# Splitting weights in steps of 1024 columns in place of 512

## The chip, the cores and the metric

The kernel runs on one core of one Trainium2 chip. The metric is the device time of one execution in microseconds (us). Its engines go by the names of the profile: PE (TensorE, the matmuls, with PEld its weight loads), DVE (VectorE), ACT (ScalarE), POOL (GpSimd) and SP (SyncE, which issues the weight DMAs).

## The reference

A trunk of four decoder layers on a sequence of 256 tokens, width 1024, all in float32. Each layer has three sub-layers, and after each of them stands `x = layer_norm(ALPHA * x + f(x))`:

```python
for i in range(DEPTH):
    kind, j = i % N_MIXERS, i // N_MIXERS
    if kind == 0:
        y = swa_sink_attention(x, a_w_qkv[j], a_sinks[j], a_w_o[j], cos_a, sin_a)
    elif kind == 1:
        y = rglru_block(x, b_w_in[j], b_conv_w[j], ...)
    else:
        y = mla_attention(x, c_w_down[j], c_q_norm[j], ...)
    x = layer_norm(ALPHA * x + y, ln_g[i, 0], ln_b[i, 0])
    x = layer_norm(ALPHA * x + memory_cross_attention(x, mem_k, mem_v, x_w_q[i], x_w_o[i]), ...)
    x = layer_norm(ALPHA * x + conv_glu_ffn(x, f_w_up[i], f_conv_w[i], f_conv_b[i], f_w_down[i]), ...)
```

The mixers are a sliding-window attention of 16 heads in 4 groups with learned sinks (layers 0 and 3), a recurrent block with real gates, the RG-LRU (layer 1), and a latent attention (layer 2). Cross-attention has 4 heads over 256 memory tokens; the FFN has 2816 gated channels with a causal convolution of width 3.

## The kernel before, in words

**Weights in two parts.** A float32 product is built from three matmuls on rounded operands: each weight and each activation is split into a high part and a low part, the difference, and high by high, high by low and low by high are summed in PSUM (`mm3`). For activations `split` (L370, L371) does this: a copy on ACT writes the high part (`xh`, `oh`, `ph`, `gh`), a subtract on DVE the low part (`xl`, `ol`, `pl`, `gl`). For weights it is the class `Weights`. `PLAN` lists the weights in pieces, most of 2048 columns on 128 partitions (1 MB), in the order in which they are used. `load` starts the DMA of a piece into one of `NRAW` = 3 buffers (`raw`) on SP's queue; `step` splits the next columns of the piece at hand: a cast on ACT into `whi` (L287), then a subtract on DVE into `wlo` (L288). There are `NSPLIT` = 4 pairs of `whi` and `wlo`; a piece's first step waits until `free` has given a pair back, that is, until PE has used it. With a piece's last step its raw buffer is given back and the next load is issued.

**When a step is issued.** The matmuls on weights go through `bulk`, which adds each one's columns / 2.4 to a credit (`tick`). When the credit has reached `STEP_NS` and no `hold` stands, one step is issued and `STEP_NS` taken off. The credit is capped at twice `STEP_NS`:

```python
def tick(self, ns):
    self.ns = min(self.ns + ns, 2 * STEP_NS)
    if self.ns >= STEP_NS and not self.hold and self.step():
        self.ns -= STEP_NS
```

`get` also issues steps, where a piece is asked for that isn't split yet. The size of a step is `PART` columns, or what is left of the piece; the first two pieces of all have sizes of their own (`FIRST`). At the end of a sub-layer `OutProj.finish` sets `hold` during the norm, so that no step is issued into its chain.

**The order of the rest.** Within a sub-layer the work of all engines is written out in short stages, and strings of tokens (`SWA_SEQ`, `RG_SEQ`, `MLA_SEQ`, `X_SEQ`), played by `play`, set the order of the stages: in the sliding window `K` turns the keys (copies to `kT`, L773), `R` applies the rotation (`ropet`, `ropeu`, L685 to L689), `U` turns the queries (`qT`, L699), `S` makes the scores, their row maxima on DVE (L722), the sink's maximum and its negative (L725, L726) and the exponentials on ACT (L731), `N` normalizes (L737 to L740), `T` turns the probabilities (`pt`, L750), `P` multiplies them with the values and splits the result into `oh` and `ol`, `C` is a part of the output projection. Cross-attention has the same stages, with the row maxima at L1090, the exponentials at L1093, and queries (`q`) and probabilities (`ph`, `pl`) split as well; `mkh`, `mvh` and their low parts are the memory's keys and values. All engines run their own instructions in order. A scheduler at build time orders them for each engine from the order of issue and its own estimate, so that a change in the steps can also move other instructions.

The change and the steps of the prediction touch `Weights.step` and `Weights.tick` with their two constants, L239 and L329; `bulk`, which calls `tick`, is at L354.

Of the kernel before, what the change touches and what calls it, by code (L numbers as in the profile page):

```python
# [235 lines left out]
MORE_REST = ((0, 2, 4), (1, 0, 4))  # L236
NRAW = 3
NSPLIT = 4
PART = 512  # L239


class Weights:
# [28 lines left out]
    def step(self):  # L271
# [9 lines left out]
        hi, lo = self.tiles[k]  # L281
        c = slice(self.part, FIRST[k][self.part] if k < 2 else min(n, self.part + PART))
        raw = self.raw[k]
# [39 lines left out]
# [3 lines that stand above are left out]
            self.ns -= STEP_NS  # L326


STEP_NS = 1200.0  # L329
XF_AT = 4  # L330
FIRST = [{0: 256, 256: 512, 512: 1024, 1024: 1536, 1536: 2048}, {0: 512, 512: 1024, 1024: 2048}]

# [945 lines left out]
```

## Time and profile before

| what | value |
|---|---|
| three runs, median (lowest to highest) | 1385.0 us (1384.55 to 1385.14) |
| the profiled execution | 1384.68 us |
| its span, first to last instruction | 1382.7 us |
| mean granted clock of TensorE | 0.999 |
| busy: PE, PEld | 99%, 89% of the span |
| busy: DVE, ACT | 78%, 64% of the span |
| DMA read over the span | 244 MB, 177 GB/s |

The times are those of the whole execution; the span leaves out what lies before the first and after the last instruction, 2.0 us here. "Busy" is the time in which an engine had an instruction in work; matmuls are pipelined, so a busy PE is not yet a PE at its peak. A granted clock of 1 is 2.4 GHz. In a timeline row the number in brackets is the idle time of the engine just before the instruction, and what ended it; a row with x4 stands for four instructions in a row, and its duration reaches from the first one's start to the last one's end.

### The profile page before, as it was taken

The page shows a single profiled execution, that of the slowest core. Times are in us where ns is not written, and L with a number is a line of the kernel's source. Part 1 is how long each engine was busy: PE and PEld are TensorE (multiplying, and loading weights), DVE is VectorE, ACT ScalarE, POOL GpSimd, SP SyncE. Part 2 cuts the span into 40 slices and gives each one's busy share as a digit, 9 for nine tenths or more (in the row PEclk, how much of TensorE's full clock was granted, in tenths as well). Part 3 has the DMA queues.
Part 4 walks back from the last instruction along what each step waited for, and adds up shares of the span by engine and source line. Part 5 has one row for each costly group of instructions (what it writes and reads, how often), then busy time and mean ns, then how long its engine had stood idle before and what let it go on. Part 6 is the DMA issues. An engine that isn't in the chain of part 4 may idle for free.

```text
span 1382.7 us, 23749 instructions
## 1 busy us (share of the span) xinstructions
PE 1363.8 (99%) x9110; PEld 1232.0 (89%) x9110; DVE 1084.8 (78%) x2392; ACT 881.1 (64%) x1892; POOL 13.0 (1%) x28
## 2 busy tenths in 40 slices
PE   8999999999999999999999999999999999999997
PEld 8887989999898898999988898999998789899996
DVE  6887869777788878877778687977779867797775
ACT  6666747555579666655557664855565856675553
POOL 0000000000000000000000000000000000000000
PEclk9999999999999999999999999999999999999999
DMA  8733536555535554655526442555554326455550
GB/s 319 273 137 122 203 104 246 205 189 183 183 123 184 199 196 168 225 187 183 179 103 236 153 176 99 214 214 185 192 195 148 135 94 228 166 214 183 185 182 31
DMA packets 39393, 246.78 MB, mean 178 GB/s; under 512 B 4336, under 2 KB 6640, under 8 KB 12400
## 3 DMA queue, kind: packets, MB, share of 16 engines
q1 hardware_dynamic: 35824, 232.69, 46.3%
q0 software_dynamic: 3456, 12.58, 2.7%
q8 instruction: 71, 1.16, 0.3%
q14 instruction: 42, 0.34, 0.1%
HBM read 244.21 MB, written 1.05 MB: 177 GB/s over the span
## 4 chain that ended last, share of the span: by engine, by line
PE 92%; ACT 3%; DVE 3%; issue 0%; DMA 0%; SPq 0%; DVEq 0%; ACTq 0%
PE ps L352 89%; PE ps L359 3%; ACT p L731 2%; DVE p L722 1%; DVE wlo L288 1%; DMA raw<-in_w_dram 0%; DVE tt L834 0%; ACT whi L287 0%; DVE x L478 0%; DVE x L480 0%; DVE x L454 0%; DVE tt L832 0%; ACT oh L370 0%; ACT tt L861 0%; DVE ropet L689 0%
## 5 line engine op out<-in xcount | busy, mean ns | idle before, releaser
L288 DVE TENSOR_TENSOR wlo<-raw,whi 128x512 fp32r<-128x512 f32 (+1 forms) x869 | 559.1, 683 | 149.5 <-ACT whi L287 143.0
L287 ACT CAST whi<-raw 128x512 fp32r<-128x512 f32 (+1 forms) x869 | 485.9, 619 | 174.6 <-PE ps L352 150.2
L352 PE MATMUL ps<-xh,whi 128*128 128x256 f32 x1504 | 421.2, 280 | 0.0
L352 PE MATMUL ps<-xh,wlo 128*128 128x256 f32 x1504 | 420.1, 279 | 0.0
L352 PE MATMUL ps<-xl,whi 128*128 128x256 f32 x1504 | 419.8, 279 | 0.0
L352 PEld LDWEIGHTS ps<-xl,whi 128*128 128x128 f32 x1504 | 282.7, 188 | 1.9
L352 PEld LDWEIGHTS ps<-xh,whi 128*128 128x128 f32 x1504 | 282.7, 188 | 1.8
L352 PEld LDWEIGHTS ps<-xh,wlo 128*128 128x128 f32 x1504 | 282.6, 188 | 0.0
L1151 DVE SCALAR_TENSOR_TENSOR cv<-ps,part,cv 128x255 f32<-128x255 f32 (+1 forms) x352 | 166.3, 477 | 3.8 <-ACT cv L1149 1.4
L352 PE MATMUL ps<-whi,xh 128*128 128x512 f32 (+3 forms) x336 | 118.4, 353 | 0.4 <-ACT xh L370 0.2
L352 PE MATMUL ps<-wlo,gh 128*128 128x512 f32 x352 | 116.0, 396 | 0.0
L352 PE MATMUL ps<-whi,gh 128*128 128x512 f32 x352 | 115.9, 396 | 0.0
L352 PE MATMUL ps<-wlo,xh 128*128 128x512 f32 (+3 forms) x336 | 115.7, 345 | 0.0
L352 PE MATMUL ps<-whi,gl 128*128 128x512 f32 x352 | 115.1, 393 | 0.0
L1149 ACT ACTIVATE cv<-ps,part 128x256 f32<-128x256 f32 x176 | 98.3, 563 | 16.9 <-DVE cv L1151 5.5
L370 ACT CAST gh<-cv 128x256 fp32r<-128x256 f32 x88 | 35.7, 406 | 107.2 <-DVE cv L1166 107.0
L352 PE MATMUL ps<-whi,oh 128*128 128x512 f32 x256 | 92.9, 403 | 3.4 <-ACT oh L370 3.4
L352 PE MATMUL ps<-whi,xl 128*128 128x512 f32 (+3 forms) x336 | 92.6, 347 | 0.0
L352 PE MATMUL ps<-wlo,oh 128*128 128x512 f32 x256 | 90.8, 394 | 0.0
L352 PE MATMUL ps<-whi,ol 128*128 128x512 f32 x256 | 90.6, 395 | 0.0
L352 PEld LDWEIGHTS ps<-whi,gl 128*128 128x128 f32 x352 | 66.3, 188 | 15.8
L352 PEld LDWEIGHTS ps<-wlo,gh 128*128 128x128 f32 x352 | 66.4, 189 | 15.3
(227 smaller groups left out, 1842.1 us busy)
## 6 DMA issues: line engine op xcount, KB each, us to landing
raw<-in_w_dram SPq DMA_DIRECT2D x210, 1024.0 KB, 4.8
lng<-in_ln_g_dram POOLq DMA_DIRECT2D x12, 512.0 KB, 4.5
lnb<-in_ln_b_dram POOLq DMA_DIRECT2D x12, 512.0 KB, 6.2
raw<-in_w_dram SPq DMA_DIRECT2D x5, 768.0 KB, 4.7
raw<-in_w_dram SPq DMA_DIRECT2D x5, 256.0 KB, 6.1
raw<-in_w_dram SPq DMA_DIRECT2D x2, 640.0 KB, 3.7
xf<-in_xT_dram SPq DMA_DIRECT2D x1, 1024.0 KB, 8.6
x<-in_x_dram SPq DMA_DIRECT2D x1, 1024.0 KB, 13.2
```

The source lines that it names most:

```text
L287: self.nc.scalar.copy(out=hi[:, c], in_=raw[:, c])
L288: self.nc.vector.tensor_tensor(out=lo[:, c], in0=raw[:, c], in1=hi[:, c].bitcast(F32), op=ALU.subtract)
L352: T.matmul(o, lhsT=l, rhs=r, start=st, stop=sp, **kw)
L359: T.transpose(o, i, ident)
L370: a = A.copy(out=hi, in_=src)
L722: V.tensor_tensor_reduce(out=pr[:, hd], in0=sc[e][:, c], in1=mk, scale=1.0, scalar=-3e38, op0=ALU.add, op1=ALU.max, accum_out=m[:, tb, hd: ...
L731: last[0] = A.activation(out=pr[:, hd], in_=pr[:, hd], func=AF.Exp, scale=A_D ** -0.5, bias=nm[:, b, hd:hd + 1], accum_out=sm[:, b, hd:hd ...
L1149: A.activation(out=dst, in_=src, func=AF.Identity, scale=wc[:, taps - 1:taps], bias=bias)
L1151: V.scalar_tensor_tensor(out=dst[:, d:], in0=src[:, :S - d], scalar=wc[:, taps - 1 - d:taps - d], in1=dst[:, d:], op0=ALU.mult, op1=ALU.add)
```

## The change

Two constants are doubled: the columns of a split step and the credit at which one is issued. A piece of 2048 columns takes two steps instead of four; one of 1536 takes 1024 and 512, one of 1280 takes 1024 and 256. The cap on the credit, which is written as twice `STEP_NS`, doubles with it.

```diff
--- before.py
+++ after.py
@@ -236,7 +236,7 @@
 MORE_REST = ((0, 2, 4), (1, 0, 4))
 NRAW = 3
 NSPLIT = 4
-PART = 512
+PART = 1024
 
 
 class Weights:
@@ -326,7 +326,7 @@
             self.ns -= STEP_NS
 
 
-STEP_NS = 1200.0
+STEP_NS = 2400.0
 XF_AT = 4
 FIRST = [{0: 256, 256: 512, 512: 1024, 1024: 1536, 1536: 2048}, {0: 512, 512: 1024, 1024: 2048}]
```

How this moves instructions is seen at two places. The first is VectorE at the beginning of the sliding window in layer 0, the difference of the orders; `wlo` is a split step, the rest the rotation of the queries:

```order
 L689 TENSOR_TENSOR ropet<-ropet,ropeu 128x512
-L288 TENSOR_TENSOR wlo<-raw,whi 128x512 x3
+L288 TENSOR_TENSOR wlo<-raw,whi 128x1024
 L685 TENSOR_TENSOR ropet<-ps,cont 128x512
 L687 TENSOR_TENSOR ropeu<-ps,cont 128x8x32 x2
-L288 TENSOR_TENSOR wlo<-raw,whi 128x512
+L288 TENSOR_TENSOR wlo<-raw,whi 128x1024
 L689 TENSOR_TENSOR ropet<-ropet,ropeu 128x512
```

Nothing has changed places here, but the single step between the rotation's products and their sum, and so ahead of the row maxima that follow, has grown from 512 columns to 1024. In the same layer, on the same engine, the row maxima of the third group end in this way before:

```order
L288 TENSOR_TENSOR wlo<-raw,whi 128x512
L725 SCALAR_TENSOR_TENSOR m<-m,sinkt 128x8
L722 ISA p_1186,m<-ps,cont 128x128
L722 ISA m 128x1
L726 TENSOR_SCALAR nm<-m 128x8
L727 TENSOR_TENSOR es<-sinkt,m 128x8
```

and in this way with the change:

```order
L288 TENSOR_TENSOR wlo<-raw,whi 128x1024
L725 SCALAR_TENSOR_TENSOR m<-m,sinkt 128x8
L722 ISA p_1126,m<-ps,cont 128x128
L722 ISA m 128x1
L726 TENSOR_SCALAR nm<-m 128x8
L727 TENSOR_TENSOR es<-sinkt,m 128x8
```

The step ahead of the sink's maximum is 1024 columns long, where it had 512. The second place is the cross-attention of layer 0. On ScalarE:

```order
 L370 CAST ph<-ps 128x512
 L1093 ACTIVATE xp,xsm<-ps,xnm 128x256 x2
-L287 CAST whi<-raw 128x512
+L287 CAST whi<-raw 128x1024
+L370 CAST ph<-ps 128x512
 L370 CAST q<-ps 128x512
-L370 CAST ph<-ps 128x512
-L287 CAST whi<-raw 128x512 x2
-L370 CAST oh<-ps 128x512
-L370 CAST ph<-ps 128x512
-L287 CAST whi<-raw 128x512
+L287 CAST whi<-raw 128x1024
```

The cast behind the exponentials has twice the columns, and the probabilities' high part now comes ahead of the query's. TensorE follows that in the same place:

```order
 L352 MATMUL ps<-mkh,q 128x256
 L352 MATMUL ps<-mkl,q 128x256
+L352 MATMUL ps<-ph,mvh 128x256
+L352 MATMUL ps<-pl,mvh 128x256
+L352 MATMUL ps<-ph,mvl 128x256
+L352 MATMUL ps<-ph,mvh 128x256
+L352 MATMUL ps<-pl,mvh 128x256
+L352 MATMUL ps<-ph,mvl 128x256
+L352 MATMUL ps<-ph,mvh 128x256
 L352 MATMUL ps<-mkh,q 128x256 x2
 L352 MATMUL ps<-mkl,q 128x256
```

Seven matmuls on the probabilities stand behind the first two on the queries, where they followed all of these.

## Rows read from the trace of the kernel before

**Rows 1.** The page, parts 1 and 4: busy time, and the chain by engine.

```profile
PE 1363.8 (99%) x9110; PEld 1232.0 (89%) x9110; DVE 1084.8 (78%) x2392; ACT 881.1 (64%) x1892; POOL 13.0 (1%) x28
...
PE 92%; ACT 3%; DVE 3%; issue 0%; DMA 0%; SPq 0%; DVEq 0%; ACTq 0%
```

**Rows 2.** Windows: us, then busy us and count by engine, PEclk, DMA share, GB/s.

```profile
83.00:112.00 29.00, 27.15 (x210) 21.43 (x209) 26.57 (x109) 25.84 (x90) 0.00 (x0) 1.00 0.29 105
428.00:448.00 20.00, 18.32 (x131) 16.62 (x129) 16.45 (x28) 18.31 (x31) 0.00 (x0) 1.00 0.30 111
211.00:380.00 169.00, 169.00 (x1194) 157.65 (x1193) 133.32 (x268) 105.62 (x216) 0.00 (x0) 1.00 0.55 198
```

**Rows 3.** Waits of PE: line <- releaser: us, times, longest us.

```profile
PE ps L352 <- ACT whi L287: 5.0, 2, 4.2
PE ps L352 <- ACT oh L370: 3.4, 4, 1.2
PE ps L359 <- DVE p L740: 1.9, 4, 0.5
```

**Rows 4.** The page, part 5: the group of the subtracts.

```profile
L288 DVE TENSOR_TENSOR wlo<-raw,whi 128x512 fp32r<-128x512 f32 (+1 forms) x869 | 559.1, 683 | 149.5 <-ACT whi L287 143.0
```

**Rows 5.** Timeline of ACT, then DVE, near the start: start us, us, operation.

```profile
15.23 1.05 ACT L287 CAST whi<-raw 128x1024 fp32r<-128x1024 f32 x1
16.44 2.19 ACT L287 CAST whi<-raw 128x512 fp32r<-128x512 f32 x4
...
16.31 1.23 DVE L288 TENSOR_TENSOR wlo<-raw,whi 128x1024 fp32r<-128x1024 f32 x1 [0.52 <-ACT whi L287]
17.79 1.89 DVE L288 TENSOR_TENSOR wlo<-raw,whi 128x512 fp32r<-128x512 f32 x3
```

**Rows 6.** Timelines of layer 0, 83 to 89 us: ACT, PE, DVE, ACT.

```profile
83.41 0.62 ACT L287 CAST whi<-raw 128x512 fp32r<-128x512 f32 x1 [3.45 <-issue]
...
84.57 2.93 PE L352 MATMUL ps<-kT,qT 64*128 64x128 f32 x32
...
84.64 0.68 DVE L288 TENSOR_TENSOR wlo<-raw,whi 128x512 fp32r<-128x512 f32 x1
...
88.76 0.40 ACT L731 ACTIVATE p<-p,nm 128x128 f32<-128x128 f32 x1 [1.71 <-DVE nm L726]
```

**Rows 7.** The same, 98 to 112 us: DVE, ACT, PE.

```profile
98.78 0.68 DVE L288 TENSOR_TENSOR wlo<-raw,whi 128x512 fp32r<-128x512 f32 x1
...
102.38 0.69 DVE L288 TENSOR_TENSOR wlo<-raw,whi 128x512 fp32r<-128x512 f32 x1
...
103.53 0.40 ACT L731 ACTIVATE p<-p,nm 128x128 f32<-128x128 f32 x1 [1.02 <-DVE es L727]
...
111.43 0.73 PE L352 MATMUL ps<-whi,oh 128*128 128x512 f32 x2 [0.73 <-ACT oh L370]
```

**Rows 8.** Timeline of DVE, sliding window of layer 3.

```profile
1095.63 0.69 DVE L288 TENSOR_TENSOR wlo<-raw,whi 128x512 fp32r<-128x512 f32 x1
```

**Rows 9.** Timelines of the first cross-attention: ACT, DVE, PE.

```profile
163.47 0.62 ACT L287 CAST whi<-raw 128x512 fp32r<-128x512 f32 x1 [0.81 <-ACT xp L1093]
...
164.13 0.69 DVE L288 TENSOR_TENSOR wlo<-raw,whi 128x512 fp32r<-128x512 f32 x1 [0.61 <-ACT whi L287]
...
165.34 0.68 DVE L371 TENSOR_TENSOR pl<-ps,ph 128x512 fp32r<-128x512 f32 x1
...
165.90 0.40 PE L352 MATMUL ps<-mkh,q 128*128 128x256 f32 x2
```

**Rows 10.** Timelines of the RG-LRU: ACT, PE.

```profile
425.64 2.18 ACT L287 CAST whi<-raw 128x512 fp32r<-128x512 f32 x4
...
441.67 0.72 PE L352 MATMUL ps<-whi,oh 128*128 128x512 f32 x2 [1.21 <-ACT oh L370]
```

**Rows 11.** Timelines of the latent attention: DVE, PE.

```profile
742.07 3.69 DVE L288 TENSOR_TENSOR wlo<-raw,whi 128x512 fp32r<-128x512 f32 x6
...
743.85 0.28 PE L352 MATMUL ps<-ckh,wlo 128*128 128x256 f32 x1
```

## Prediction

> **What bounds the kernel now.** I read the busy line of the page and its chain first. TensorE is busy for 1363.8 of 1382.7 us and its lines make up 92% of the chain; VectorE is at 78%, ScalarE at 64% [rows 1]. The windows show the same by stage: in the FFN stretch from 211 to 380 us TensorE is busy for all 169.00 us while VectorE and ScalarE have slack, at a granted clock of 1.00, which is the 2.4 GHz level. In the sliding-window stage of layer 0, from 83 to 112 us, TensorE is busy for 27.15 of 29 us, and VectorE (26.57) and ScalarE (25.84) are nearly as full [rows 2]. So the split steps are hidden wherever TensorE has long runs of matmuls, and they are queued in the way only in the short chains of softmax and gates. The waits of TensorE say how much is lost there. The 5.0 us for the first whi are the start-up, whose two pieces have step sizes of their own that the change leaves alone; behind it stand 3.4 us for oh and 1.9 us for p, 5.3 us in all [rows 3]. That is nearly all that a better order of VectorE and ScalarE could win back; no such limit stands against a loss.
>
> **What the change costs, part by part.** *The instructions.* 869 pairs of cast and subtract [rows 4] become 442 by the order of the new program: 428 of 1024 columns, 10 of 512 and four of 256. A single 512 step costs 0.62 us on ScalarE [rows 6] and 0.68 on VectorE [rows 8]; in a row each further one adds (2.19-0.62)/3 = 0.52 and (1.89-0.68)/2 = 0.60. A step of 1024 took 1.05 and 1.23 us at the one place that has it [rows 5]. So one step of 1024 is 0.62+0.52-1.05 = 0.09 us cheaper than two of 512 on ScalarE, and 0.68+0.60-1.23 = 0.05 us on VectorE. Some 427 merges give about 38 and 21 us of busy time. Neither engine sets the pace, so I count this at nothing; TensorE's own runs hide it. If they did not, ScalarE and VectorE would have 36% and 22% of the span in reserve.
>
> The Trainium skill ("VectorE: DVE Perf Modes", section "The TRN2 errata") speaks for the larger step: it says that an fp32 tensor_tensor of N columns takes (N+151)/0.96 ns and that many small tiles pay the fixed part each time, while one large tile pays it once. Its durations, 691 and 1224 ns, agree with the rows; but by it a merge would save 157 ns, an estimate, where the back-to-back rows leave 50. By either figure the sum here stays as it is.
>
> *The wait in front of others.* What counts is the other side. An operation queued behind one step now stands 1.05-0.62 = 0.43 us longer behind a cast and 1.23-0.68 = 0.55 longer behind a subtract. Steps are half as many, so this hits half as often; where a single 512 stood in front of something urgent and a 1024 stands there now, it is a loss.
>
> *Sliding window, layer 0.* The cast at 83.41 stands before the copies of kT that the score matmuls at 84.57 take, and the subtract at 84.64 between ropeu and ropet, ahead of the row maxima [rows 6]; both become 1024 in the new order. The scores come 0.43 later and the maxima 0.55, so the first exponential at 88.76 starts about 0.55 late, and ScalarE then runs its exponentials without a gap. Three 512 subtracts before the normalization become one 1024, which frees 0.6 us on VectorE, but by then the sums come from ScalarE, so that does not help. The subtract at 98.78 and the one at 102.38 [rows 7], both ahead of the third group's negated maximum, also become 1024: twice 0.55 more. The exponentials at 103.53, which waited 1.02 us for VectorE, start 3 x 0.55 = 1.65 later; ScalarE runs them without a gap, and the oh cast behind them is what TensorE waited for at 111.43. I take +1.7 us; bounds 0.5 (only the first delay comes through) and 2.2 (with a further 0.5 from one cast).
>
> *Sliding window, layer 3.* The beginning is the same: +0.5. But in the third group the subtract at 1095.63 [rows 8] and another right behind the sink's maximum, 2 x 0.6 us, move out of the chain in the new order, which pays for the two steps that grew before them; the beginning's delay stays. I take +0.5, bounds -0.7 and +1.2.
>
> *Cross-attention, four times.* The cast at 163.47 starts after an idle 0.81 us that the profile puts down to ScalarE itself, long done; I take it for the wait for a free pair, and so for one that stays. The subtract behind it started at 164.13, when the cast had ended; then came q's low part and, at 165.34, the second pl [rows 9]. Now the cast ends at 163.47+1.05 = 164.52, its subtract at 164.56+1.23 = 165.79, and pl, which the order puts next, about 166.4. The order also brings seven matmuls on ph and pl ahead of the second mkh,q matmuls, so that pl is wanted in the place of the second of the pair at 165.90 [rows 9]: about 166.0, since a pair takes 0.40 us there and one such matmul 0.28 [rows 11]. That is a new wait of 0.4 us. The low part of q, now behind pl at 167.0, is wanted after seven matmuls of some 0.12 us from there, 167.1, and is just in time. Four layers: +1.6, bounds 0 (pl's subtract gets ahead after all) and 2.4 (0.6 each).
>
> *RG-LRU.* From 428 to 448 us ScalarE is busy for 18.31 of 20 us [rows 2], with four casts in a row at 425.64, as many 5.7 us later, and then the oh that TensorE waits 1.21 us for at 441.67 [rows 10]. Four casts of 1024 for the eight are 4 x 0.09 us shorter; a subtract ahead of the second oh is 0.5 longer. I take 0, bounds -1.0 and +0.5.
>
> *Latent attention.* Six subtracts run from 742.07; the second ends at 742.07+0.60+0.68 = 743.35, and the matmul at 743.85 is among the first to use such a weight [rows 11]: 0.5 us of slack. A first 1024 step ends at 742.07+1.23 = 743.30, still in time. I take +0.1, bounds -0.3 and +0.6.
>
> *The rest.* The FFNs (TensorE has no gap there), the transfers (a raw buffer is freed after the same columns, and the DMA engines are at a share of 0.29 to 0.55 [rows 2]), the norms and the tail without any step: 0.
>
> The sum is 1.7+0.5+1.6+0+0.1 = +3.9 us on the profiled execution's 1384.7 us, hence 1388.6; the median of the three runs, 1385.0, lies 0.3 above that execution, and I leave that out.
>
> **The rivals.** (A, the forecast) The larger step stands longer before urgent work: 1388.6.
>
> (B) The cover holds. TensorE waits for weights in no place behind the start-up [rows 3], the cross waits do not arise since pl is done first, and of layer 0's three delays one is caught up by the shorter row before the normalization. Left: about 0.9+0.5 us, 1386.0. For it speaks that no row shows TensorE waiting in a cross stage now; against it, that the margin there is only a few tenths.
>
> (C, the other side) Fewer instructions shorten the full chains. If the three-for-one before the normalization (1.89-1.23 = 0.66 us a layer) and the four-for-eight before oh decide, rather than the single steps that grew, the 5.3 us of waits [rows 3] shrink: all gone would be 1379.4, two thirds 1381.2. It decides if the first maxima wait for the scores rather than for the subtract at 84.64 by more than 0.55 us. The rows speak against it: VectorE goes from subtract to maxima without a gap. The skill's rule above is on this side; by its fixed part a merge would be worth three times as much.
>
> (D) Weights come late. A 1024 step ends only when its second half is done; where the slack is 0.5 us [rows 11], a step that had been cut between two matmul groups now ends up to 0.6 late. Five such places on top of A give 1391.5. Against it: the list of waits has none of this kind behind the start-up [rows 3], so that all the slack must go first.
>
> That the change does not do what it says is ruled out by the counts above: only the start and the ends of seven odd pieces keep small steps.
>
> **How the numbers follow.** A measurement of this kernel can tell about 0.2%, 2.8 us, from no change, so "same" is 1382.2 to 1387.8. Chances: A 0.47, B 0.33, C 0.10, D 0.10. A's own bounds reach from 1386.5 to 1390.5, so a small part of it, about 0.05, falls under the limit: faster 0.10, same 0.38, slower 0.52. The range runs from 1384.0, under B with the gains of RG-LRU and layer 3, to 1391.3, which takes in A's cross bound and the start of D; it leaves out C and most of D, under 0.2.
>
> **What would show it.** Right: TensorE waits for pl in each cross stage, some 0.4 us, where there is none now; the waits for oh grow from 3.4 us to above 4.5; the stretch from 83 to about 113 us is longer by 1.7, and the exponentials at 103.53 start near 105.2; FFN stretches keep their length. Wrong: no wait on pl (B), shorter waits for p and oh (C), waits for whi or wlo behind the start-up (D), or a change in the matmuls' pace within the FFNs, which nothing here foresees.

## The result: 7 us slower, where 3.6 were forecast

| | before | after |
|---|---|---|
| six runs, median | 1384.78 us | 1391.79 us |
| lowest to highest | 1384.18 to 1385.48 us | 1390.65 to 1393.67 us |
| the profiled execution, its span | 1384.68, 1382.7 us | 1392.59, 1390.6 us |

The ratio is 1.0052, with an interval from 1.0042 to 1.0061. The direction was forecast; the size lies 0.5 us above the range, which ended at 1391.3. One execution of those below, with the change in the FFNs alone, took 2252.13 us at a mean granted clock of 0.558; it stands outside every comparison.

The page after the change, its busy line, its chain by engine and the groups of subtracts and casts (columns as ahead of the prediction):

```profile
PE 1365.7 (98%) x9110; PEld 1231.9 (89%) x9110; DVE 1059.0 (76%) x1965; ACT 843.6 (61%) x1465; POOL 13.0 (1%) x28
...
PE 89%; ACT 5%; DVE 4%; issue 1%; DMA 1%; SPq 0%; DVEq 0%; ACTq 0%
...
L288 DVE TENSOR_TENSOR wlo<-raw,whi 128x1024 fp32r<-128x1024 f32 (+1 forms) x442 | 520.6, 1201 | 165.2 <-ACT whi L287 162.7
L287 ACT CAST whi<-raw 128x1024 fp32r<-128x1024 f32 (+1 forms) x442 | 443.3, 1034 | 188.2 <-PE ps L352 163.9
```

The edit did what it says: 442 subtracts for 869 [rows 4]. VectorE lost 1084.8-1059.0 = 25.8 us of work and ScalarE 37.5, close to the 21 and 38 of the prediction, and TensorE got slower all the same. In the chain TensorE's share fell from 92% to 89% while ScalarE and VectorE rose from 3% each to 5% and 4% [rows 1]: TensorE waits for them more often. The waits of TensorE after the change, all that the view lists:

```profile
PE ps L352 <- ACT whi L287: 5.7, 2, 4.4
PE ps L352 <- ACT oh L370: 4.5, 4, 1.8
PE ps L352 <- ACT cqh L922: 2.3, 1, 2.3
PE ps L359 <- DVE p L740: 2.1, 4, 0.6
PE ps L352 <- DVE pl L371: 1.0, 4, 0.3
PE ps L352 <- ACT kT L773: 0.7, 2, 0.4
PE ps L352 <- ACT xh L370: 0.4, 1, 0.4
PE ps L352 <- ACT pt L750: 0.4, 2, 0.2
PE ps L352 <- DVE wlo L288: 0.2, 1, 0.2
```

Against [rows 3], oh rose by 1.1 us; pl is new, as forecast, and so is kT, where the scores were to come 0.43 us later. The wait for cqh, which the prediction did not name, stands at 2.3 us; in the same view of the kernel before it is

```profile
PE ps L352 <- ACT cqh L922: 0.4, 1, 0.4
```

Where the time went is seen when the starts of the same matmul, by its number among the 9110 of each trace, are subtracted; the sum is that of the spans, 7.9 us:

| stretch | after minus before, us |
|---|---|
| start-up, to the first sliding window | -1.5 |
| sliding window, layer 0 | +1.6 |
| cross-attention, layers 0 to 3 | +0.95, +0.84, +0.76, +1.0 |
| the four FFNs | 0 |
| RG-LRU | -0.4 |
| norm ahead of the latent attention | +0.3 |
| latent attention | +3.95 |
| sliding window, layer 3 | +0.44 |

The start-up is not a gain to count on. Its first steps are the same in both kernels; between 10 and 13.3 us the matmuls of 256 columns start 0.21 us apart in the trace of before and 0.12 us apart in that of the change, which makes the 1.5 us. In the profiles of the experiments below the same stretch came out between -1.0 and +0.9 us.

**Cross-attention.** VectorE and then TensorE in the first of the four, the rows that answer to [rows 9]:

```profile
165.07 1.23 DVE L288 TENSOR_TENSOR wlo<-raw,whi 128x1024 fp32r<-128x1024 f32 x1 [1.46 <-ACT whi L287]
166.21 0.68 DVE L371 TENSOR_TENSOR pl<-ps,ph 128x512 fp32r<-128x512 f32 x1
...
166.95 0.39 PE L352 MATMUL ps<-pl,mvh 128*128 128x256 f32 x1 [0.25 <-DVE pl L371]
```

This is the chain that was worked out: cast, subtract of 1.23 us, pl, and a matmul that waits for pl.

**Latent attention.** The chain of waits after the change there (start us, us, what), and the matmul at its end:

```profile
728.67 6.58 DMA raw<-in_w_dram
735.24 0.02 issue
735.26 1.05 ACT whi L287
736.31 0.38 ACT cqh L922
736.69 0.04 issue
736.74 3.31 PE ps L352 x13
...
736.74 0.38 PE L352 MATMUL ps<-cqh,whi 128*128 128x256 f32 x1 [2.30 <-ACT cqh L922]
```

No matmul waits for that weight. But its cast stands ahead of cqh in ScalarE's order, it waits for its transfer, and then takes 1.05 us. In the trace of before the same place reads as follows (ScalarE):

```profile
731.98 0.61 ACT L287 CAST whi<-raw 128x512 fp32r<-128x512 f32 x1
732.49 1.21 ACT L922 ACTIVATE cqh<-ps,part 128x256 fp32r<-128x256 f32 x3
```

There the cast found its weights landed, since no idle time stands in its row, and TensorE waited 0.4 us for cqh. Behind the long wait of the changed kernel comes a second loss. Its windows (columns as in [rows 2]):

```profile
736.00:739.00 3.00, 2.26 (x10) 1.68 (x11) 2.59 (x7) 3.00 (x10) 0.00 (x0) 0.89 0.56 235
739.00:742.00 3.00, 3.00 (x16) 3.00 (x15) 3.00 (x9) 1.97 (x3) 0.00 (x0) 0.54 0.32 44
742.00:745.00 3.00, 3.00 (x15) 2.37 (x14) 2.39 (x13) 0.59 (x1) 0.00 (x0) 1.00 0.73 309
```

The mean granted clock of the window from 739 us is 0.54, so for most of it the lower level of 1.2 GHz was granted, behind a wait of TensorE of 2.3 us; from 742 us it is 1.00 again. From the end of the wait to that point the lag behind the trace of before grows from 3.7 to 5.5 us, by another 1.7 us.

### The profile page after: what moved, and what is told of

The parts are those of the page before. It is cut to its first block, busy times and chain, and to the rows that moved or that the text cites. A ratio compares the mean times of both kernels' runs of the same rounds, so it can differ in the third digit from the quotient of the medians.

```text
span 1390.6 us, 22907 instructions
## 1 busy us (share of the span) xinstructions
PE 1365.7 (98%) x9110; PEld 1231.9 (89%) x9110; DVE 1059.0 (76%) x1965; ACT 843.6 (61%) x1465; POOL 13.0 (1%) x28
## 3 DMA queue, kind: packets, MB, share of 16 engines
HBM read 244.21 MB, written 1.05 MB: 176 GB/s over the span
## 4 chain that ended last, share of the span: by engine, by line
PE 89%; ACT 5%; DVE 4%; issue 1%; DMA 1%; SPq 0%; DVEq 0%; ACTq 0%
PE ps L352 86%; PE ps L359 3%; ACT p L731 2%; DVE wlo L288 2%; ACT whi L287 1%; DVE p L722 1%; DMA raw<-in_w_dram 0%; DMA memf<-in_memT_dram 0%; DVE tt L834 0%; ACT xp L1093 0%; DVE x L478 0%; ACT L1093 0%; DVE tt L832 0%; DVE pl L371 0%; DVE x L480 0%
## 5 line engine op out<-in xcount | busy, mean ns | idle before, releaser
L288 DVE TENSOR_TENSOR wlo<-raw,whi 128x1024 fp32r<-128x1024 f32 (+1 forms) x442 | 520.6, 1201 | 165.2 <-ACT whi L287 162.7
L287 ACT CAST whi<-raw 128x1024 fp32r<-128x1024 f32 (+1 forms) x442 | 443.3, 1034 | 188.2 <-PE ps L352 163.9
L352 PEld LDWEIGHTS ps<-whi,gh 128*128 128x128 f32 x352 | 63.9, 189 | 11.9
```

Source lines behind the costliest of these rows:

```text
L287: self.nc.scalar.copy(out=hi[:, c], in_=raw[:, c])
L288: self.nc.vector.tensor_tensor(out=lo[:, c], in0=raw[:, c], in1=hi[:, c].bitcast(F32), op=ALU.subtract)
L352: T.matmul(o, lhsT=l, rhs=r, start=st, stop=sp, **kw)
```

## The experiments

The theory: a step is paid for where a single longer instruction stands ahead of urgent work on ScalarE or VectorE, in the sliding windows, in cross-attention and in the latent attention. The rivals: the loss is spread over all larger steps; it comes from the rarer and larger portions, not from the length of an instruction; the transfers alone make the wait for cqh. Changes against the kernel before ("+4.4") are medians of runs on the same chip, in us.

**Undo the change in one kind of stage.** Step size and credit became variables of `Weights`, set ahead of each stage:

```diff
-        c = slice(self.part, ... min(n, self.part + PART))
+        c = slice(self.part, ... min(n, self.part + self.size))
...
+SIZES = {"cross": (512, 1200.0)}
...
+        W.size, W.per = SIZES.get(kind, (PART, STEP_NS))
         rest = scoped(run[kind], i, rest)
```

> The changed kernel, but split steps of 512 columns at a credit of 1200 while the four cross-attentions are issued; 1024 and 2400 elsewhere. By the theory that the time goes where a longer step stands ahead of urgent work, each cross stage gives back its two waits (about 0.2 for xp and 0.5 behind pl, 0.8 us with what follows): 4 x 0.8 = 3.3 us, from 1391.8 to about 1388.5, and no wait of TensorE for pl is left. By the rival that the loss is spread evenly over all larger steps, the cross stages hold about one seventh of them and the time comes to 1390.8.

1388.86 against 1384.44: +4.4, ratio 1.0032 (1.0019 to 1.0044). The whole change costs 0.52% of 1384.44, 7.2 us, so the four cross stages held 7.2-4.4 = 2.8 us; TensorE has no wait for pl any more. By the two intervals such a difference is uncertain by some 2 us either way, here and in the next two runs.

> The changed kernel, but split steps of 512 columns at a credit of 1200 while the two sliding-window mixers are issued. By the theory of urgent work behind longer steps layer 0 gives back 1.6 us and layer 3 0.5 us: about 1389.7, the wait for kT goes and the wait for oh in layer 0 is 0.9 us again. By the rival of an even spread these stages hold some 7% of the steps: 1391.3.

1389.18: +4.7, ratio 1.0034 (1.0021 to 1.0046), 2.5 us given back. The wait for kT is gone, that for oh is 3.5 us in all.

> The changed kernel, but split steps of 512 columns at a credit of 1200 while the latent attention is issued. By the theory that the long wait for cqh comes from a cast of 1024 that stands ahead of it and has to wait for its whole transfer, and the low granted clock behind it from that wait, both go: 2.0 us of wait and 1.6 us of clock, about 1388.2, and the granted clock is 0.999 in every run. By the rival that the transfer is late because of the steps before this stage, the wait stays at about 2 us and the time at 1391.5.

1389.85: +5.4, ratio 1.0041 (1.0028 to 1.0054). Only 1.8 of the 3.6 us came back in the median, and the interval overlaps that of the whole change, so that this run alone does not show it. In the profile the wait for cqh is 0.4 us: a part of the 3.95 us belongs to the one execution that was profiled. And the clock did fall, in another place. The windows of this run around the sliding window of layer 0, where TensorE had just waited 1.84 us for oh:

```profile
108.00:112.00 4.00, 2.36 (x11) 1.58 (x9) 2.46 (x6) 4.00 (x19) 0.00 (x0) 1.00 0.01 4
112.00:116.00 4.00, 3.80 (x13) 3.11 (x14) 3.00 (x5) 3.65 (x6) 0.00 (x0) 0.65 0.00 0
```

**The change in the FFNs alone** (`SIZES = {"ffn": (1024, 2400.0)}`, 512 and 1200 elsewhere).

> Steps of 1024 columns at a credit of 2400 in the four FFN stages alone, which hold over half of all steps; 512 and 1200 elsewhere. By the theory that TensorE hides the steps in its long runs the time is that of the kernel before, 1384.8 within 0.7 us. By the rival of an even spread it is about 1388.8.

1385.16, the median of ten executions: +0.7, ratio 1.0007 (0.9998 to 1.0016), which is not told from no change. An even spread, 4 us, is out. Its profile is a warning, though: with 512 steps in the latent attention TensorE waited 1.4 us for cqh, since the transfer had landed late:

```profile
733.47 0.62 ACT L288 CAST whi<-raw 128x512 fp32r<-128x512 f32 x1 [0.93 <-DMA raw<-in_w_dram]
```

**The same portions in two instructions.** At each credit of 2400 two steps of 512 are issued.

```diff
-        if self.ns >= STEP_NS and not self.hold and self.step():
+        if self.ns >= self.per and not self.hold and self.step():
+            self.step()
```

> Credit of 2400 as in the change, with its cap of 4800, but each time two steps of 512 columns are issued in place of one of 1024: the same columns as often, cut in two instructions. By the theory that the length of one instruction in front of urgent work is the price, the time is that of the kernel before, 1384.5 to 1385.5, since other instructions can go between the two, and the waits for kT and pl are gone. By the rival that the rarer, larger portions themselves (credit and cap) are the price, it stays at about 1391.5.

1384.52, as the kernel before: ratio 0.9999 (0.999 to 1.0008). Credit and cap cost nothing measurable, and the waits for kT and pl are gone: the scheduler puts other work between the two, in the first cross-attention the low parts of the query and of the probabilities. This rules out the second rival by itself.

**Loads in two halves**, with steps of 1024 and of 512.

```diff
-        for a, b in FIRST[k].items() if k < 2 else ((0, n),):
+        for a, b in FIRST[k].items() if k < 2 else ((0, 1024), (1024, n)):
```

> The changed kernel with every load of a piece cut into two transfers of at most 1024 columns, so that the first cast of a piece waits for its half alone. By the theory that the wait for cqh in the latent attention is made of a longer cast (0.5 us) and a transfer that lands late under two others (0 to 1.5 us, another in each execution), the second part goes: the wait for cqh is 1.0 us or less, no low granted clock stands behind it, and the time is about 1390.5; cross and sliding window keep their waits. By the rival that the transfer has no part in it the wait stays above 2 us and the time at 1391.6. Should more transfers cost something by themselves, the time rises above that.

> The kernel before (steps of 512, credit 1200) with the same cut of the loads. By the same theory the wait for cqh of 0.4 us goes and the slow executions lose up to 1 us: about 1384.0; without a part of the transfers 1384.5.

Both expectations fell: 1399.21 (+14.7, ratio 1.0103, 1.0089 to 1.0117) and 1388.98 (+4.5, ratio 1.0033, 1.002 to 1.0045). ScalarE's waits for weights, first with the whole loads of the change, then with halves (engine, line waited for: us, times, longest), and the page's DMA line of the latter (KB each, median us to landing):

```profile
ACT whi L287 <- DMA raw<-in_w_dram: 11.5, 12, 2.5
```

```profile
ACT whi L288 <- DMA raw<-in_w_dram: 30.5, 28, 3.5
...
raw<-in_w_dram SPq DMA_DIRECT2D x428, 512.0 KB, 4.7
```

The 4.7 us mix the two halves. Of each pair the first landed after a median of 4.0 us and the second 5.3 us after the first was issued, against 4.8 for a whole: a cast of the first half could start 0.8 us earlier, one of the second half 0.5 us later. But casts moved ahead in ScalarE's order at some places, and there they waited, with the softmax behind them: TensorE waited 2.7 us for cqh and 2.3 us for xp. With halves and steps of 512 it waited 1.0 us for cqh, where no wait was expected. The experiment changed the order as well as the transfers, and so tells less of the transfers than it was meant to; it does show once more what a cast that waits in front of others costs.

**Smaller steps** (`PART = 256`, `STEP_NS = 600.0`).

> The other direction: steps of 256 columns at a credit of 600 everywhere. By the theory of urgent work behind longer steps each single step stands 0.27 us shorter in the way, which gives some 1 us back in the sliding windows; against it stand twice as many instructions, whose fixed cost fills ScalarE in the recurrent block (some 0.1 us for each step more, about 1 us there). Expected 1384.5, between 1383.0 and 1386.0. By the rival that fewer instructions are what counts it is well slower, above 1388.

1388.34: +3.8, ratio 1.0026 (1.0016 to 1.0037). The expectation fell, and the time is that of its rival, by which fewer instructions are what counts. In its profile the recurrent block, with the norm behind it, takes 2.0 us more, the wait for cqh is 1.4 us, and that for p grew from 1.9 to 2.4 us. Of 256, 512 and 1024 columns everywhere, 512 is the best.

**Which engine's instruction is it?** Casts of 1024 with subtracts in two instructions of 512, and the reverse:

```diff
-            self.nc.vector.tensor_tensor(out=lo[:, c], in0=raw[:, c], ...)
+            for h in parts:
+                self.nc.vector.tensor_tensor(out=lo[:, h], in0=raw[:, h], ...)
```

> The changed kernel (credit 2400) with casts of 1024 columns, but each subtract in two instructions of 512. By the theory each engine's own longer instruction has its own price. What comes from the cast stays: the wait for kT (0.4 us in each sliding window) and the longer cast ahead of cqh in the latent attention. What comes from the subtract goes: the wait for pl in the four cross stages, since pl would be ready at 164.56+0.60+0.68 = 165.85, before it is wanted, and some 1 us of the wait for oh in layer 0. About 1388.3. By the rival that the cast is the whole price (the subtract only follows it) it stays at 1391.

> The other half: two casts of 512 columns, one subtract of 1024. By the theory the wait for kT goes, and cqh waits behind 512 columns alone; the subtract of 1024 still stands ahead of the third group's exponentials in layer 0 (0.5 us and more) and of pl where it comes first. About 1387.0, between 1385.5 and 1389. By the rival that the cast is the whole price it is 1384.8; by the rival that the subtract is the whole price, 1391.

1389.43 (+4.9, ratio 1.0038, 1.0025 to 1.005) and 1388.06 (+3.5, ratio 1.0029, 1.0017 to 1.004), each 1.1 us above the expectation. Either half alone costs, so neither engine's instruction is the whole price. They add up to 8.4 us against 7.2 for both; with intervals of over 1 us on each, that is not told from a plain sum. The casts alone leave the wait for kT (0.7 us) and none for pl. The subtracts alone leave no wait for kT; TensorE then waits 3.2 us for p. In both, the order happened to put the cast behind cqh. ScalarE in the second:

```profile
733.58 0.38 ACT L897 ACTIVATE junk<-ps 128x256 f32<-128x256 f32 x1
...
733.96 1.20 ACT L927 ACTIVATE cqh<-ps,part 128x256 fp32r<-128x256 f32 x3
735.02 0.49 ACT L898 ACTIVATE rr<-ss,epsl 128x1 f32<-128x1 f32 x2
735.39 2.19 ACT L291 CAST whi<-raw 128x512 fp32r<-128x512 f32 x4
```

The transfer took 6.22 us here, nearly as long as the 6.58 us of the changed kernel, and TensorE waited 0.3 us for cqh. So in this profile a late transfer cost nothing at cqh, with the cast of its weights behind cqh.

No run changes the length of the steps with the order of all other instructions held. In the second of these two, TensorE's order in the first cross-attention is that of the kernel before, pl's subtract goes ahead of the weight's, and TensorE does not wait for pl. So the wait for pl in the changed kernel can't be put down to the longer step alone: the order that came with it has a part.

**The change in the latent attention alone.**

> The kernel before with steps of 1024 at a credit of 2400 in the latent attention alone. By the theory its longer cast makes cqh 0.5 us later for sure and more where a transfer lands late: the wait for cqh is 0.9 us or more, the time about 1386.3, and executions differ by more than in the kernel before (over 2 us). By the rival that what happens before this stage makes the wait, it is 0.4 us as before and the time 1384.6.

1386.53: +2.0, ratio 1.0018 (1.0009 to 1.0027), with executions from 1385.17 to 1388.89. It agrees with the 1.8 us of the opposite experiment, and here the interval is clear of no change. In the profile, where the first transfer landed after 5.2 us, TensorE waited 0.9 us for cqh.

**All three places undone together.**

> The changed kernel with steps of 512 at a credit of 1200 in sliding window, cross-attention and latent attention together; 1024 and 2400 stay in the FFNs, the recurrent block and at the start. By the theory the three places hold the whole loss and add up: single undoings gave back 2.8, 2.5 and 1.8 us of some 7.1, so the time is that of the kernel before, 1384.5, between 1383.5 and 1385.5. By the rival that one wait hides another, or that the late transfers in the stages behind the FFNs take a part whatever the steps there, 1 to 2 us are left: 1386.

1385.0 against 1384.88: ratio 0.9998 (0.9989 to 1.0007). Larger steps stay at the start, in the FFNs and in the recurrent block, and no loss is left beyond some 1 us, the width of the interval. The waits of TensorE in its profile:

```profile
PE ps L354 <- ACT whi L288: 5.2, 2, 4.2
PE ps L354 <- ACT oh L372: 3.5, 4, 1.0
PE ps L361 <- DVE p L742: 1.9, 4, 0.5
PE ps L354 <- ACT cqh L924: 0.4, 1, 0.4
PE ps L354 <- ACT pt L752: 0.3, 2, 0.2
```

No version came out measurably faster than the kernel before.

## Why the prediction was wrong in size

**Bound and instructions: right.** The FFN stretches kept their length and their pace of matmuls, and 63 us of work saved on ScalarE and VectorE bought nothing.

**Sliding windows: right.** +1.7 and +0.5 were forecast; the two traces differ by 1.6 and 0.44, the undoing gave back 2.5. From the first exponential of layer 0 to that of the third group the trace of before has 103.53-88.76 = 14.77 us [rows 6, 7]; now it has 15.87:

```profile
87.79 0.41 ACT L731 ACTIVATE p<-p,nm 128x128 f32<-128x128 f32 x1 [2.43 <-DVE nm L726]
...
103.66 0.40 ACT L731 ACTIVATE p<-p,nm 128x128 f32<-128x128 f32 x1 [2.12 <-DVE es L727]
```

That is twice 0.55, as worked out; the third 0.55 lies ahead of the first row.

**Cross-attention: the mechanism right, the size half.** The term of 0.4 us a stage took only pl. The matmul that takes pl now starts 0.42 us later than TensorE's pace would give, so that part was sized well; but 0.2 us more are lost earlier in each stage, where a subtract of 1024, in place of one of 512, stands between the row maximum (L1090) and its scaling (L1091) and delays the exponentials, and 0.1 to 0.2 in small gaps around. The four stages measured 2.8 us (undone) to 3.5 us (the traces), where 1.6 were forecast and 2.4 was the upper bound.

**RG-LRU: a little better than forecast**, -0.4 for 0; the gain is in the norm behind it, where TensorE waits less for xh.

**Latent attention: the step that failed.** It was priced at +0.1, with 0.6 as the bound, from the slack of weights at their first use [rows 11]. That asked whether TensorE gets its weight in time, and it does: behind the start-up it waits for none (the 0.2 us for wlo lie at 9.5 us). The step did not ask what stands behind the cast on ScalarE. It was the question that was put in the sliding window and in cross-attention, and not here, though the view of waits had cqh with 0.4 us in the line below those of [rows 3]. The stage cost 2.0 us (the change there alone) and 1.8 us (undone there), and 3.95 in the profiled execution, with a late transfer and the low clock. The profiles of four kernels that have steps of 1024 in this stage, and the cast ahead of cqh, tell the parts from each other. In all four the norm ahead takes some 0.35 us more than before. Where the first transfer landed after 5.2 us (512 in the sliding windows; the change in this stage alone), the stage itself takes 1.0 us more; where it landed after 6.1 us (512 in cross-attention) 3.3, and after 6.6 us (the changed kernel) 3.95, with the low clock in both. So some 1.4 us are there without a late transfer, and up to 3 more come with one. With steps of 512 in the stage a late transfer alone cost 1.0 us (the change in the FFNs).

With the terms as measured by undoing, 2.8+2.5+1.8 = 7.1 us, the sum is that of the comparison, 7.0 to 7.2; each term is uncertain by some 2 us, and the run with all three undone is the firmer test of the whole. The forecast's own upper bounds, 2.2+1.2+2.4+0.5+0.6 = 6.9 us, lie above its range and just below the measured 7.0. What an execution adds is not settled in every part: the first of three transfers that are in flight together there landed after 4.9 to 5.3 us in some profiles and after 6.1 to 6.6 in others, and no run shows what decides between the two.

**The rivals.** B and C are ruled out for this change by its time: half as many instructions came out slower. That more of them cost nothing does not follow, as the steps of 256 show (+3.8 us). (B's and D's sums are 1386.1 and 1391.6, 0.1 us above what was written.) D came nearest in time and named the late weights, but the wrong victim: not TensorE, but the work behind the cast. The rule of the Trainium skill ("VectorE: DVE Perf Modes", section "The TRN2 errata") on the fixed part of each instruction agrees with the durations here (0.68 and 1.23 us), and it is about work, not about waiting; by work alone the change is a gain of 63 us, by the time of the kernel a loss of 7.

## What to carry to other kernels

On an engine that runs in order, the size of background work is a latency for whatever stands behind it: choose it by the tightest chain it is threaded into, not by its cost per column. Stages with long runs of matmuls bear a longer step than stages with short chains; here sizes of their own avoided the loss but gained nothing (1385.0 against 1384.88). To price such an edit, list for every chain stage the background instruction directly ahead of each operation that TensorE waits for, and ask two things: how much longer is it, and what does it itself wait for (a transfer above all). Two instructions of half the length are not the same as one, since a scheduler can put urgent work between them. Steps can also be too small: with 256 columns the kernel was 3.8 us slower than with 512.

## What the runs showed of the hardware

- The granted clock fell to the level of 1.2 GHz within some 2 us of the end of single waits of TensorE (2.30 us for cqh after the change; 1.84 us for oh in the third experiment; 1.84 us for cqh in the first) and stayed there for about 3 us each time; the wait of 1.80 us for oh in the changed kernel left it at 1.00.
- Transfers of 512 KB, issued in pairs 0.37 us apart, landed after a median of 4.7 us, those of 1 MB after 4.8 us; the first of a pair landed after 4.0 us.
- Back to back, a 512-column subtract follows the last after 0.60 us, though one takes 0.68: merging two saves 0.05 us. The Trainium skill ("VectorE: DVE Perf Modes", section "The TRN2 errata") would give 0.157 us by its fixed part, an estimate; the measurement decides.
